# The loads of the running sequences' states are issued by GpSimd in place of SyncE

## The chip, the cores and the metric

The kernel runs on one core of one Trainium2 chip. The time is the device time of one execution in microseconds (us), as a median over several runs. Five engines work side by side, each through its own instructions in order: TensorE (PE), VectorE (DVE), ScalarE (ACT), GpSimd (POOL) and SyncE (SP). They wait for one another by semaphores. A transfer between the main memory and SBUF is issued by an instruction on one of the engines and then runs on 16 transfer engines.

## The reference

One layer of a hybrid decoder is computed for two inputs at once: a prompt of 512 new rows with 16 meta rows ahead, and eight running sequences of eight new rows each, which bring their states with them. The part that matters here is the state scan (SSD) of the running sequences: each sequence has for each of 32 heads a state of 64 x 128 numbers, which enters the outputs and is carried on.

```
def step(h, inp):
    x, d, bc, cc = inp
    cum = jnp.cumsum(d * a_g, axis=1)
    ...
    y = jnp.einsum('btsgh,bsghp->btghp', m, xdt)
    y = y + jnp.einsum('btgn,bghpn->btghp', cc, h) * jnp.exp(cum)[..., None]
    last = cum[:, -1]
    xw = xdt * jnp.exp(last[:, None] - cum)[..., None]
    h = h * jnp.exp(last)[..., None, None] + jnp.einsum('bsgn,bsghp->bghpn', bc, xw)
    return h, y
```

`h` starts as `state_ssm` of the sequence. Around the scan stand an input projection, pooling and convolution mixers, gates, an output projection and a feed-forward part, all in float32.

## The kernel before, in words

All 592 columns (16 meta, 512 prompt, 64 of the running sequences) lie transposed, features on partitions. Every product with a weight matrix is a `Unit`: the weights are loaded (line 95, tile `wr`, two buffers), split into a high part `wh` on ACT (line 113) and a low part `wl` on DVE (line 114), and multiplied in three passes (lines 119 to 121) into PSUM tiles `mm`. PE is fed with such units through the whole program, and the scan is woven between them: `weave` puts the steps of `ssd_steps(g)`, g = 0 to 3, between the units in program order. So there are four groups of eight heads each, in the text the first to the fourth. A scheduler then orders the instructions of each engine by its own estimate of when they can run.

In one group the steps that touch the change are these. `local(c)` loads the running sums of one chunk of rows (`cumD`, line 709), combines them on DVE (line 712), takes eight exponentials on ACT (line 714), multiplies them with the scores (DVE line 720), and reads the scores' PSUM tile a last time on ACT (line 723). `carry(c)` multiplies the chunk's operands (PE line 773). The PSUM tiles `px` that all these products and transposes use come from a ring of five, so a product may have to wait until an engine has read an older tile. `sample_load(u)`, u = 0 and 1, loads the states of four sequences in four transfers of 256 KB, each 128 partitions by four rows of 512 bytes, into two tiles `t` (line 793): the first and the second load of the group. `sample_turn(u)` transposes them on PE (line 804) into PSUM and copies them out on ACT (line 805). `sample_in`, `sample_add` and `sample_out` use them; `sample_out` scales the loaded states in place (ACT line 861), adds the new part (DVE line 862) after the products of line 857, and stores them (line 864). The tiles `t` come from a ring of nine buffers that the whole scan shares, so each load waits until the buffer's last reader is done.

GpSimd's own work in this stretch is small: it clears and fills the edges of the convolution's tiles `ext` (lines 630 and 631, three buffers), saves their ends (line 637), adds the carried part to the outputs (line 783) and adds up squares (line 926). All loads and stores but four stand in SyncE's queue.

Of the kernel before, what the change touches and what calls it, by code (L numbers as in the profile page):

```python
# [35 lines left out]
def hybrid_step(  # L36
# [8 lines left out]
    V, S, G, PE, DMA = nc.vector, nc.scalar, nc.gpsimd, nc.tensor, nc.sync  # L45
# [14 lines left out]
    def slot(shape, dt=F32):  # L60
        return sp.tile(shape, dt, tag="T", bufs=9, name=nm("t"))
# [618 lines left out]
    def rows_of(state, b, hs):  # L680

        return state[0, b, hs].rearrange("h p n -> (h p) n").rearrange("(j q) n -> q j n", q=128)

    def ssd_steps(g):

        hs = slice(8 * g, 8 * g + 8)
# [100 lines left out]
        def sample_load(u):  # L787

            h0s = []
            for i in range(2):  # L790
                t = slot([128, 2, 4, 128])
                for b in range(2):
                    DMA.dma_start(out=t[:, b], in_=rows_of(state_ssm, 4 * u + 2 * i + b, hs))
                h0s.append(t)
            st["h0", u] = h0s

# [84 lines left out]
        for c in range(1, 5):  # L881
            u = (c - 1) // 2
            if c % 2:
                steps.append(go(sample_load, u))
            if c < 4:
                steps.append(go(local, c))
            steps += [go(ahead, c), go(inside, c - 1)]
            if c % 2:
                steps += [go(sample_turn, u), go(carry, c - 1), go(sample_x, u)]
            else:  # L890
                steps += [go(sample_in, u), go(carry, c - 1), go(sample_add, u), go(sample_out, u)]
# [353 lines left out]
    for h in range(2):  # L1245
        for m in (6, 7):
            u = last[m]
# [35 lines left out]
```

## Time and profile before

| | us |
|---|---|
| runs, median of 3 | 1240.4 |
| runs, lowest and highest | 1239.92 and 1241.38 |
| the profiled execution, its own time | 1237.16 |
| the profiled execution, its span | 1235.4 |
| TensorE busy in the span | 1215.4 |
| VectorE busy in the span | 778.0 |
| GpSimd busy in the span | 168.2 |

The span runs from the first to the last instruction. The time of an execution is a little longer than its span. Busy time of TensorE is that of its matmuls, which overlap one another in the pipeline; what counts here is where it is idle. Issues of transfers do not count as busy time of an engine.

### The profile page before, as it was taken

The page shows a single profiled execution, that of the slowest core. Times are in us where ns is not written, and L with a number is a line of the kernel's source. Part 1 is how long each engine was busy: PE and PEld are TensorE (multiplying, and loading weights), DVE is VectorE, ACT ScalarE, POOL GpSimd, SP SyncE. Part 2 cuts the span into 40 slices and gives each one's busy share as a digit, 9 for nine tenths or more (in the row PEclk, how much of TensorE's full clock was granted, in tenths as well). Part 3 has the DMA queues.
Part 4 walks back from the last instruction along what each step waited for, and adds up shares of the span by engine and source line. Part 5 has one row for each costly group of instructions (what it writes and reads, how often), then busy time and mean ns, then how long its engine had stood idle before and what let it go on. Part 6 is the DMA issues. An engine that isn't in the chain of part 4 may idle for free.

```text
span 1235.4 us, 22605 instructions
## 1 busy us (share of the span) xinstructions
PE 1215.4 (98%) x9148; PEld 1176.3 (95%) x9148; DVE 778.0 (63%) x1372; ACT 557.0 (45%) x1164; POOL 168.2 (14%) x325
## 2 busy tenths in 40 slices
PE   8999999999999999999999999999999999999996
PEld 6999999899899989989999999999999999999996
DVE  6875347578888989787743344367676325677634
ACT  5435343545566577566442224344334113334333
POOL 2410000012013013011100001321212000111100
PEclk8999999999999999999999999999999999999999
DMA  6334426662634455654553542223322223222322
GB/s 187 109 78 123 117 89 192 173 184 51 185 115 122 135 164 141 178 151 140 156 146 100 170 139 70 69 69 103 103 69 70 85 86 103 68 69 85 113 74 77
DMA packets 174456, 143.99 MB, mean 117 GB/s; under 512 B 11630, under 2 KB 163854, under 8 KB 174345
## 3 DMA queue, kind: packets, MB, share of 16 engines
q1 hardware_dynamic: 173969, 142.40, 39.2%
q8 instruction: 72, 1.18, 0.4%
q14 instruction: 31, 0.25, 0.1%
q10 hardware_dynamic: 384, 0.16, 0.0%
HBM read 122.42 MB, written 20.34 MB: 116 GB/s over the span
## 4 chain that ended last, share of the span: by engine, by line
PE 92%; DMA 4%; ACT 2%; DVE 1%; SPq 1%; issue 0%; ACTq 0%; DVEq 0%
PE mm L119 27%; PE mm L121 27%; PE mm L120 27%; DMA t<-in_x_prompt_dram 1%; PE px L764 1%; PE px L742 1%; DMA t<-in_state_ssm_dram 1%; PE px L773 1%; DMA t<-cumD 1%; PE px L804 1%; ACT t L714 1%; PE px L817 1%; PE px L857 1%; PE px L726 1%; PE px L119 1%; PE px L121 1%
## 5 line engine op out<-in xcount | busy, mean ns | idle before, releaser
L119 PE MATMUL mm<-s,wl 128*128 128x288 f32 (+5 forms) x2528 | 759.4, 300 | 1.9 <-ACT s L297 1.4
L120 PE MATMUL mm<-s,wh 128*128 128x288 f32 (+5 forms) x2528 | 750.9, 297 | 0.0
L121 PE MATMUL mm<-s,wh 128*128 128x288 f32 (+5 forms) x2272 | 677.2, 298 | 0.0
L119 PEld LDWEIGHTS mm<-s,wl 128*128 128x128 f32 (+1 forms) x2528 | 476.0, 188 | 8.6 <-issue 5.3
L120 PEld LDWEIGHTS mm<-s,wh 128*128 128x128 f32 (+1 forms) x2528 | 476.1, 188 | 3.9 <-issue 3.3
L121 PEld LDWEIGHTS mm<-s,wh 128*128 128x128 f32 (+1 forms) x2272 | 427.3, 188 | 1.9 <-issue 1.4
L114 DVE TENSOR_TENSOR wl<-wr,wh 128x1024 fp32r<-128x1024 f32 (+2 forms) x165 | 198.5, 1203 | 169.5 <-ACT wh L113 169.0
L113 ACT ACTIVATE wh<-wr 128x1024 fp32r<-128x1024 f32 (+2 forms) x165 | 170.5, 1033 | 239.8 <-PE mm L121 196.7
L121 PE MATMUL mm<-t,wh 128*128 128x290 f32 (+1 forms) x256 | 76.0, 297 | 0.0
L1131 DVE SCALAR_TENSOR_TENSOR acc<-ext,ffT,acc 128x592 f32<-128x592 f32 x88 | 74.2, 844 | 1.7 <-ACT acc L1129 0.2
L642 DVE SCALAR_TENSOR_TENSOR acc<-ext,scT,acc 128x616 f32<-128x616 f32 x72 | 63.4, 880 | 1.9 <-ACT acc L640 1.4
L714 ACT ACTIVATE t<-t,TK 128x128 f32<-128x128 f32 (+1 forms) x160 | 48.5, 385 | 22.9 <-DVE t L712 22.9
L926 POOL TENSOR_TENSOR sqs<-sqs,acc 128x578 f32<-128x578 f32 x19 | 31.3, 1648 | 142.1 <-ACT acc L925 76.7
L121 PEld LDWEIGHTS mm<-t,wh 128*128 128x128 f32 x256 | 48.1, 188 | 0.0
L1158 ACT ACTIVATE s<-ext 128x512 fp32r<-128x512 f32 (+1 forms) x44 | 17.1, 436 | 64.3 <-DVE ext L1154 64.3
L861 ACT ACTIVATE t<-t,spr 128x128 f32<-128x128 f32 x128 | 40.2, 394 | 7.9 <-PE px L804 7.7
L1122 DVE TENSOR_TENSOR ext<-mm,t 128x224 f32<-128x224 f32 x43 | 16.8, 391 | 40.7 <-PE mm L121 40.7
L783 POOL TENSOR_TENSOR s<-s,tmp 128x256 f32<-128x256 f32 (+1 forms) x32 | 35.0, 1113 | 53.3 <-DVE tmp L777 45.7
L1159 POOL TENSOR_TENSOR s<-ext,s 128x512 fp32r<-128x512 f32 (+1 forms) x44 | 37.3, 870 | 34.9 <-ACT s L1158 34.9
L1184 DVE TENSOR_TENSOR t<-t,mm 128x288 f32<-128x288 f32 (+2 forms) x30 | 13.6, 453 | 43.6 <-PE mm L121 43.4
L1125 POOL COPY t<-ext 128x18 f32<-128x18 f32 x44 | 11.4, 259 | 202.4 <-DVE ext L1123 202.3
L1129 ACT ACTIVATE acc<-ext,ffT 128x592 f32<-128x592 f32 x44 | 38.1, 869 | 1.6 <-DVE ext L1123 1.5
(290 smaller groups left out, 1269.7 us busy)
## 6 DMA issues: line engine op xcount, KB each, us to landing
wr<-in_w_in_dram SPq DMA_DIRECT2D x28, 1024.0 KB
wr<-in_w_up_dram SPq DMA_DIRECT2D x22, 1024.0 KB
t<-cumD SPq DMA_DIRECT2D x16, 512.0 KB
t<-in_state_ssm_dram SPq DMA_DIRECT2D x32, 256.0 KB
out_dram<-t SPq DMA_DIRECT2D x32, 256.0 KB
wr<-in_w_ssd_out_dram SPq DMA_DIRECT2D x8, 1024.0 KB
wr<-in_w_down_dram SPq DMA_DIRECT2D x8, 768.0 KB
wr<-in_w_in_dram SPq DMA_DIRECT2D x10, 512.0 KB
```

The source lines that it names most:

```text
L113: S.activation(wh[:, :kb, :n], wr, AF.Copy)
L114: V.tensor_tensor(wl[:, :kb, :n], wr, f(wh[:, :kb, :n]), ALU.subtract)
L119: PE.matmul(o, wl[:, k, :m], hi[:, a:b], start=first, stop=False)
L120: PE.matmul(o, wh[:, k, :m], hi[:, a:b], start=False, stop=False)
L121: PE.matmul(o, wh[:, k, :m], lo[:, a:b], start=False, stop=last)
L642: V.scalar_tensor_tensor(acc[:, 0:616], ext[:, k:k + 616], scT[:, kb, 24 + k:25 + k], acc[:, 0:616], op0=ALU.mult, op1=ALU.add)
L714: S.activation(seg[:q, h, :q], seg[:q, h, :q], AF.Exp, scale=-1.0, bias=sums_[:, h:h + 1])
L783: G.tensor_tensor(v, v, t1[:, 2 * i:2 * i + 2, :nt], ALU.add)
L861: S.activation(v[:, b], v[:, b], AF.Copy, scale=elS[:, 4 * u + 2 * i + b, 4 * g + j:4 * g + j + 1])
L1129: S.activation(acc[:, 0:w], ext[:, 0:w], AF.Identity, scale=ffT[:, kb, 16:17], bias=ffT[:, kb, 19:20])
L1131: V.scalar_tensor_tensor(acc[:, 0:w], ext[:, k:k + w], ffT[:, kb, 16 + k:17 + k], acc[:, 0:w], op0=ALU.mult, op1=ALU.add)
L1159: G.tensor_tensor(l, a, f(h), ALU.subtract)
```

## The change

The four transfers of `sample_load` are issued by `G` (GpSimd) and no longer by `DMA` (SyncE).

```
             for i in range(2):
                 t = slot([128, 2, 4, 128])
                 for b in range(2):
-                    DMA.dma_start(out=t[:, b], in_=rows_of(state_ssm, 4 * u + 2 * i + b, hs))
+                    G.dma_start(out=t[:, b], in_=rows_of(state_ssm, 4 * u + 2 * i + b, hs))
                 h0s.append(t)
             st["h0", u] = h0s
```

Both queues are in order, so a load now waits its turn among other instructions than before, and the scheduler places some other instructions anew. Three places show it.

SyncE in the second group, around the group's first load. `wr_4076` is a block of weights, `t_3762` and `t_3765` are the two tiles of states, `t_3768` and `t_3981` are running sums of the chunks:

```order
 L709 DMA t_3662<-cumD 128x1024
 L95 DMA wr_4076<-in_w_in_dram 128x8x256
-L793 DMA t_3762<-in_state_ssm_dram 128x4x128 x2
-L793 DMA t_3765<-in_state_ssm_dram 128x4x128 x2
 L709 DMA t_3768<-cumD 128x1024
 L754 DMA t_3864<-ecumD 64x4x128 x2
+L709 DMA t_3981<-cumD 128x1024
 L95 DMA wr_4183<-in_w_in_dram 128x8x256
```

The running sums now follow the weights directly, and the next ones come ahead of the next weights. In the first group it is alike: the running sums stood behind the weights, the four loads of states and a store of line 608; now they stand behind the weights and one load of line 604, ahead of that store.

GpSimd in the third group, around the group's first load (`t_4923` and `t_4926`); `ext` with a number is a tile of the convolution:

```order
 L631 COPY ext_5329<-scT 128x8x3
 L637 COPY s_1167<-ext_5004 128x27
+L793 DMA t_4923<-in_state_ssm_dram 128x4x128 x2
+L793 DMA t_4926<-in_state_ssm_dram 128x4x128 x2
 L630 MEMSET ext_5579 128x3
 L631 COPY ext_5579<-scT 128x8x3
```

The four issues stand behind the copy of line 637 and ahead of the next tile's filling. In the second group they stand directly behind the filling of line 631, in the fourth directly behind an addition of line 783.

TensorE in the second group, where the product of line 773 (into `px_3969`, whose buffer in the ring was that of the next chunk's scores, read last by ACT at line 723) stands in a unit of 24 matmuls on the tile `mm_4009`:

```order
 L119 MATMUL mm_4009<-s_97,wl_3861 128x296
 L120 MATMUL mm_4009<-s_97,wh_3860 128x296
+L773 MATMUL px_3969<-t_3678 128x512
+L716 MATMUL px_3992<-s_2992 128x128
+L717 MATMUL px_3992<-ident,s_2992 128x128
+L726 MATMUL px_3999<-ident,s_3206 128x128 x2
+L726 MATMUL px_3999<-ident,s_3207 128x128 x2
 L121 MATMUL mm_4009<-s_101,wh_3860 128x296
```

The product moved from near the end of the unit to near its beginning. Most of the transposes of line 804 moved ahead too, in the second, third and fourth groups.

## Rows read from the trace of the kernel before

**Rows 1.** The page's head: span, and busy time of each engine.
```profile
span 1235.4 us, 22605 instructions
...
PE 1215.4 (98%) x9148; PEld 1176.3 (95%) x9148; DVE 778.0 (63%) x1372; ACT 557.0 (45%) x1164; POOL 168.2 (14%) x325
```
**Rows 2.** Stretches: length, busy time per engine, granted clock, DMA share, GB/s.
```profile
190.00:592.00 402.00, 396.19 (x3049) 368.22 (x3049) 320.65 (x578) 240.58 (x571) 61.14 (x102) 1.00 0.54 151
326.00:329.00 3.00, 3.00 (x24) 3.00 (x23) 3.00 (x4) 1.80 (x7) 0.00 (x0) 1.00 0.02 5
...
427.00:438.00 11.00, 9.78 (x83) 9.16 (x82) 8.84 (x19) 6.48 (x18) 0.23 (x1) 1.00 0.86 240
```
**Rows 3.** Waits of PE, 190 to 592 us: total, times, longest.
```profile
PE px L804 <- DMA t<-in_state_ssm_dram: 3.7, 3, 2.1
PE px L804 <- ACT t L723: 1.2, 1, 1.2
...
PE px L773 <- ACT t L723: 0.2, 1, 0.2
```
**Rows 4.** PE's timeline: start, length, instruction, [idle before it, releaser].
```profile
224.14 0.66 PE L804 MATMUL px<-ident,t 128*128 128x128 f32 x4 [1.16 <-ACT t L723]
...
336.31 0.63 PE L804 MATMUL px<-ident,t 128*128 128x128 f32 x4 [2.11 <-DMA t<-in_state_ssm_dram]
...
343.62 0.30 PE L120 MATMUL mm<-s,wh 128*128 128x296 f32 x1
...
434.86 0.63 PE L804 MATMUL px<-ident,t 128*128 128x128 f32 x4 [1.22 <-DMA t<-in_state_ssm_dram]
...
525.13 0.63 PE L804 MATMUL px<-ident,t 128*128 128x128 f32 x4 [0.38 <-DMA t<-in_state_ssm_dram]
```
**Rows 5.** SyncE's timeline around the first loads of the groups.
```profile
206.99 3.67 SPq L793 DMA_DIRECT2D t<-in_state_ssm_dram  x4
...
213.34 0.99 SPq L709 DMA_DIRECT2D t<-cumD  x1
...
329.16 4.80 SPq L793 DMA_DIRECT2D t<-in_state_ssm_dram  x4
334.02 1.22 SPq L709 DMA_DIRECT2D t<-cumD  x1
...
426.98 4.26 SPq L793 DMA_DIRECT2D t<-in_state_ssm_dram  x4
...
518.17 4.64 SPq L793 DMA_DIRECT2D t<-in_state_ssm_dram  x4
```
**Rows 6.** Pieces of the chain that ended last: start, length, work.
```profile
305.90 0.93 PE px L857 x4
...
562.65 1.81 PE px L804 x16
```
**Rows 7.** All of lines 793 and 783: ns min/median/max, first and last start.
```profile
L793 SPq DMA_DIRECT2D t<-in_state_ssm_dram x32: 438/540/2057, 207.0 to 547.3; - x32
...
L783 POOL TENSOR_TENSOR s<-s,tmp x32: 247/1118/2921, 249.6 to 588.9; 128x256 f32<-128x256 f32 x24, 128x32 f32<-128x32 f32 x8
```
**Rows 8.** Waits of SyncE's queue at line 604 for stores.
```profile
SPq L604 <- DMA mAD<-ext: 8.5, 4, 3.1
```
**Rows 9.** GpSimd's timeline: the instructions ahead of the moved loads.
```profile
323.32 0.21 POOL L631 COPY ext<-scT 128x24 f32<-128x24 f32 x1
...
428.88 0.23 POOL L637 COPY s<-ext 128x27 f32<-128x27 f32 x1 [6.41 <-ACT ext L634]
...
503.65 1.59 POOL L783 TENSOR_TENSOR s<-s,tmp 128x32 f32<-128x32 f32 x2 [7.58 <-ACT ext L645]
```
**Rows 10.** The second group's chain (timeline), and line 861's group (page).
```profile
340.82 1.23 DVE L712 TENSOR_TENSOR t<-t,TK 128x1024 f32<-128x1024 f32 x1 [2.95 <-DMA t<-cumD]
...
346.29 0.26 ACT L723 ACTIVATE t<-px 128x128 f32<-128x128 f32 x1
...
L861 ACT ACTIVATE t<-t,spr 128x128 f32<-128x128 f32 x128 | 40.2, 394 | 7.9 <-PE px L804 7.7
```

More of the change, by code (lines that the diff above doesn't have):

```diff
@@ L792, in sample_load @@
                 for b in range(2):
-                    DMA.dma_start(out=t[:, b], in_=rows_of(state_ssm, 4 * u + 2 * i + b, hs))
+                    G.dma_start(out=t[:, b], in_=rows_of(state_ssm, 4 * u + 2 * i + b, hs))
                 h0s.append(t)
```

## The prediction

> **What bounds the kernel now.** The page's head comes first [rows 1]: TensorE (PE) is busy for 1215.4 of 1235.4 us in 9148 instructions, one every 0.13 us; GpSimd (POOL) has 14%. So the time can change only where PE stands still. The table by stretches gives PE 396.19 us of the 402 in which the four groups of the state scan run, at full granted clock [rows 2]: 5.8 us of idle time, which is all that this stretch could give back. What PE waits for there is in the table of waits [rows 3]: 3.7 us in three waits for the state loads, before the transposes of line 804; 1.2 us once at the same line for ACT at line 723; 0.2 at line 773. PE's timeline places them [rows 4]: the states 2.11 us ahead of 336.31 (second group), 1.22 ahead of 434.86 (third), 0.38 ahead of 525.13 (fourth), ACT ahead of 224.14 (first). The three belong to a group's first load of states. SyncE's queue shows why these are late [rows 5]: the states leave right behind a load of weights (line 95), which waits for its own buffer, at 329.16, 426.98 and 518.17. Their buffers had been free for long: the products of line 857, the last readers, end at 306.83 for the load of 329.16 [rows 6].
>
> **The change, part by part.** It moves 32 transfers of 256 KB from SyncE's queue to GpSimd's. The bytes and buffers are the same. What moves is the place in two in-order queues, and with it PE's order, which the scheduler rewrites.
>
> *The cost of an issue on GpSimd.* No trace here has one; call it d. From below: SyncE's own, 0.44 us at least and 0.54 in the median [rows 7]. From above: the longest instruction of GpSimd among those that run beside VectorE in this stretch, 2.92 us, against a median of 1.12 for the same line [rows 7]. I take 1.1, because an issue on GpSimd is an instruction of that engine and the median is what it mostly takes; both ends stay in the range.
>
> *First group.* The states were no bound here, and GpSimd's place for them lies ahead of SyncE's 206.99. What moves is the running sums: cumD was issued at 213.34, behind the four issues of states (3.67 us) and a store [rows 5]. In the new order it follows the weights and one load of line 604. That load waits for a store to land; the longest such wait was 3.1 us [rows 8]. So cumD goes by 206.99 + 3.1 + 0.3 = 210.4 at the latest, 2.9 us earlier, and 1.05 MB of states no longer run beside it. The chain behind cumD ends in line 723, and the fourth four of transposes needs the PSUM tile that this line reads last: 1.16 us of waiting [rows 4]. 2.9 covers it. **-1.2.**
>
> *Second loads of each group.* These wait for a product of PE in both queues, so they leave when they left before. The last was issued by 547.8 (start 547.3 plus one issue) and is read at 562.65 [rows 6, 7]: about 15 us, against at most 4 x 2.92 + 1.1 = 12.8. Zero.
>
> *Second group, first load.* GpSimd is free for it at 323.32 + 0.21 = 323.53 [rows 9], 5.6 us before SyncE was. The transfer engines were nearly empty from 326 to 329 (share 0.02) [rows 2]. At the 240 GB/s of the third group's crowded stretch [rows 2], 256 KB take 1.09 us and the whole load 4.4, so even if it only begins at 326 it is there at 330.4. PE came to the transposes at 336.31 - 2.11 = 334.2; the new order puts them five matmuls earlier, at 333.5, and the second half of the tiles is wanted at about 335.1. The wait of 2.11 us goes; this holds up to d = 2.6 (323.5 + 4d + 1.1 = 335.1).
>
> *What is late next there.* The new order puts the product of line 773 nineteen matmuls earlier, directly behind the one that started at 343.62; without the wait of 2.11 PE is there at 343.92 - 2.11 = 341.8. It needs the PSUM tile that ACT frees at line 723, and that ended at 346.55, at the end of a chain that began with cumD: line 712 started at 340.82, after waiting 2.95 us for it [rows 10]. So the chain takes 5.7 us. cumD stood behind the four state issues on SyncE (334.02). Now it follows the weights at once: 1.57 MB at 240 GB/s from about 329.7 are there at 336.2. ACT is fuller at that time: thirteen scalings of line 861 at 0.3 us each (40.2 us for 128) [rows 10] stand between 333.9 and 337.8, 0.4 us past the end of line 712, and another 0.2 I allow behind. The chain ends at 342.5, and PE waits 0.7 us. Net for this group: -2.1 + 0.7 = **-1.4**.
>
> *Third group, first load.* Here GpSimd is the later one. The load stands behind a copy (line 637) that waits for ACT and runs at 428.88 to 429.11 [rows 9]; SyncE issued at 426.98 [rows 5]. And the new order of PE asks sooner: the first transposes three matmuls earlier than 433.64, at 433.25, the third four only six matmuls and two fours of transposes on. The engines move 240 GB/s from 427 to 438 [rows 2], 2.6 MB: weights (1.05), states (1.05), cumD (0.52), and before, the states came ahead of cumD. With two queues I let them take equal turns from 430 on: half the states are there at 430 + 0.52 / 0.12 = 434.3, the other half with the last byte, at 438. PE waits 1.0, then works 1.5, and waits from 435.8 to 438: 3.2 in all against 1.22. Net **+2.0**. If the states ran ahead of cumD instead, cumD would come last, the chain behind it would end as before, and the product of line 773, which moved ahead here as well, would wait for it: about the same sum. d does not enter until 429.1 + 4d + 1.1 passes 438, at d = 1.95; from there each us of d costs 4.
>
> The Trainium skill says in "DMA: Bandwidth & Descriptors", section "Issuing engines are not separate DMA queues", that transfers from all issuing engines run on the same 16 engines and interleave, and that issuing from several saves only issue time. The share of 0.86 from 427 to 438 agrees [rows 2]. By that rule the third group is as summed; the second gains all the same, as its engines stood empty.
>
> *Fourth group, first load.* The addition before it in GpSimd's queue ends at 503.65 + 1.59 = 505.24 [rows 9], 13 us before SyncE's issue. The 0.38 goes: **-0.4**. cumD leaves SyncE some 4.6 us earlier, the length of the four issues [rows 5], so the chain to line 773 is early too.
>
> The sum is -1.2 - 1.4 + 2.0 - 0.4 = -1.0 us. The profiled execution took 1237.16 us (span 1235.4); that makes 1236.2. The median of the runs is 1240.4, so I forecast 1239.4: **no change**. About 0.2%, 2.5 us, is what a measurement can tell here.
>
> **Rivals.** *Faster:* in the third group the bytes come sooner than I sum them: the engines' share there was 0.86 and not 1, so some of the 11 us was empty, and with two issuers more is in flight. If that keeps the wait of 1.2 as it is, the sum is -3.0: 1237.4 us. At best both its wait and the 0.7 at line 773 are gone too: -1.2 - 2.1 - 1.2 - 0.4 = -4.9, 1235.5. For it: the share of 0.02 ahead of the second group shows how soon an early load is over. Against it: GpSimd issues 2.1 us later than SyncE just there.
>
> *Slower, by the issue:* descriptors written by GpSimd are held up like its other work. The same tensor operation of line 783 takes 1.12 us mostly and 2.92 at worst [rows 7]. At 2.92 the third group's second half is there at 441.9, 3.9 us later than summed; the second group's at 336.3, 1.2 late. Sum -1.0 + 3.9 + 1.2 = +4.1: 1244.5. It decides from d = 2.7, where -1.0 + 4 x (2.7 - 1.95) + 4 x (2.7 - 2.6) reaches 2.4. The Trainium skill has a rule that speaks for this rival, in "SBUF — State Buffer", section "SBUF: two separate sides": while VectorE runs an operation in a mode that takes both ports, GpSimd cannot write descriptors, and a transfer of 620 ns becomes 3100 ns. By that figure, an estimate, d is 3.1 and the sum near +5. Whether VectorE's operations here are of that kind no run so far shows.
>
> *Slower, by the order:* PE's rewritten order asks in the second group for line 723's tile 4.7 us before ACT gave it up before (341.8 against 346.55). If cumD comes no earlier, because the states now share the transfer engines with it, PE waits 4.7 instead of 0.7: +4.0, 1243.4. The empty engines before 329 speak against it.
>
> That the change does not do what it says is excluded: the order shows all 32 issues on GpSimd.
>
> **How the numbers follow.** No change 0.52; faster 0.28; slower by the issue 0.13; slower by the order 0.07. So faster 0.28, same 0.52, slower 0.20. The range runs from the best of the faster case to the worse slow one, 1235.5 to 1244.5; the likeliest case alone, with d anywhere below 2.7 and turns of any kind, is 1237.9 to 1242.9.
>
> **What would show it.** In the changed kernel's trace: d as the length of an issue on GpSimd; no wait for ACT at line 804 near 222; no wait of PE for states near 333 and 524; one of about 3 us near 434; a short wait at line 773 for ACT near 342; line 712 of the second group starting near 336 and not 341; SyncE without the 4 us of state issues behind the weights. Wrong, if issues take over 2 us, if line 773 waits for more than 2 us, or if states still land last where the engines were empty.

## The result, and the profile after

The changed kernel takes 1246.15 us (median of 6, 1244.87 to 1247.7), the kernel before 1239.86 (median of 6, 1239.05 to 1241.38). The ratio is 1.0055 (95% interval 1.0046 to 1.0065): slower by 6.3 us, and outside the predicted range. The profiled execution took 1246.6 us (span 1244.9). The one of before was a quick one for its kernel (1237.16), so the two profiles differ by 9.4 us where the medians differ by 6.3.

What PE waits for from 190 to 600 us (line waited at, releaser, total, times, longest); it answers to [rows 3]:

```profile
PE px L804 <- DMA t<-in_state_ssm_dram: 4.9, 1, 4.9
PE px L804 <- issue: 3.9, 2, 2.0
PE px L804 <- ACT t L723: 1.0, 1, 1.0
PE px L742 <- DVE t L720: 0.5, 1, 0.5
```

PE's timeline places them, as [rows 4] did before:

```profile
223.18 0.66 PE L804 MATMUL px<-ident,t 128*128 128x128 f32 x4 [0.97 <-ACT t L723]
...
341.58 0.99 PE L804 MATMUL px<-ident,t 128*128 128x128 f32 x4 [1.98 <-issue]
...
438.62 1.09 PE L804 MATMUL px<-ident,t 128*128 128x128 f32 x4 [4.88 <-DMA t<-in_state_ssm_dram]
...
529.80 1.09 PE L742 MATMUL px<-t,t 128*64 128x128 f32 x16 [0.52 <-DVE t L720]
...
538.38 0.63 PE L804 MATMUL px<-ident,t 128*128 128x128 f32 x4 [1.96 <-issue]
```

The states are late in the third group alone, and there by 4.88 us instead of 1.22. In the second and fourth groups a stop of 2 us has taken the place of the wait for states. It stands before the last four of the group's sixteen transposes, and the trace names no releaser for it ("issue"). VectorE's timeline in the second group names it:

```profile
337.94 1.23 DVE L712 TENSOR_TENSOR t<-t,TK 128x1024 f32<-128x1024 f32 x1 [2.46 <-DMA t<-cumD]
339.08 0.85 DVE L642 SCALAR_TENSOR_TENSOR acc<-ext,scT,acc 128x616 f32<-128x616 f32 x1
339.85 0.34 DVE L746 SCALAR_TENSOR_TENSOR s<-s,spr,px 128x128 f32<-128x128 f32 x1
340.11 0.86 DVE L642 SCALAR_TENSOR_TENSOR acc<-ext,scT,acc 128x616 f32<-128x616 f32 x1
340.88 0.60 DVE L746 SCALAR_TENSOR_TENSOR s<-s,spr,px 128x128 f32<-128x128 f32 x2
```

The fourth four of transposes needs the PSUM tile that the additions of line 746 read. The last of them ends at 341.48, and PE goes on at 341.58. They stand in VectorE's queue behind line 712, which waited 2.46 us for cumD. Before, the scheduler had them ahead of line 712, which started at 340.82 [rows 10]:

```profile
337.52 0.34 DVE L746 SCALAR_TENSOR_TENSOR s<-s,spr,px 128x128 f32<-128x128 f32 x1
```

With each of the three stops the granted clock falls to the lower level, 1.2 GHz (in the third group it falls while PE still stands). In the table by stretches (length, busy times, granted clock, DMA share, GB/s) the kernel before showed 1.00 [rows 2], and read microsecond by microsecond it is 1.00 from 190 to 600; now:

```profile
342.00:345.00 3.00, 3.00 (x14) 3.00 (x13) 2.62 (x5) 3.00 (x9) 0.25 (x2) 0.50 0.00 0
...
439.00:442.00 3.00, 3.00 (x16) 2.97 (x15) 0.67 (x3) 1.97 (x6) 0.00 (x0) 0.50 0.06 18
...
539.00:542.00 3.00, 3.00 (x17) 3.00 (x16) 2.19 (x3) 3.00 (x11) 0.00 (x0) 0.61 0.00 0
```

PE is busy there, but at 0.5 three us do about the work of 1.5. How much each group lost is read from its second set of transposes, which wait for nothing in either kernel. PE's timeline of before, first of each group:

```profile
271.55 1.64 PE L804 MATMUL px<-ident,t 128*128 128x128 f32 x13
...
372.57 0.66 PE L804 MATMUL px<-ident,t 128*128 128x128 f32 x4
...
468.69 0.66 PE L804 MATMUL px<-ident,t 128*128 128x128 f32 x4
...
562.51 1.95 PE L804 MATMUL px<-ident,t 128*128 128x128 f32 x16
```

and of the changed kernel:

```profile
271.51 1.75 PE L804 MATMUL px<-ident,t 128*128 128x128 f32 x14
...
373.02 1.09 PE L804 MATMUL px<-ident,t 128*128 128x128 f32 x8
...
474.52 0.66 PE L804 MATMUL px<-ident,t 128*128 128x128 f32 x4
...
572.16 1.95 PE L804 MATMUL px<-ident,t 128*128 128x128 f32 x16
```

The changed kernel stands at 0.0, +0.5, +5.8 and +9.7 us: the first group cost nothing, the second 0.5, the third 5.4, the fourth 3.8.

GpSimd's timeline shows the issues themselves (compare [rows 9]):

```profile
323.83 2.98 POOL L793 DMA_DIRECT2D t<-in_state_ssm_dram  x4 [0.34 <-issue]
...
429.99 2.98 POOL L793 DMA_DIRECT2D t<-in_state_ssm_dram  x4 [0.39 <-issue]
...
511.55 2.99 POOL L793 DMA_DIRECT2D t<-in_state_ssm_dram  x4
```

and the row of line 793 answers to [rows 7] (ns, shortest, median and longest):

```profile
L793 POOL DMA_DIRECT2D t<-in_state_ssm_dram x32: 747/749/967, 191.3 to 556.5; - x32
```

An issue takes 0.75 us, at most 0.97. So d was not the cost.

### The profile page after: what moved, and what is told of

Its sections match the earlier page's. It is cut to its first block, busy times and chain, and to the rows that moved or that the text cites. A ratio compares the mean times of both kernels' runs of the same rounds, so it can differ in the third digit from the quotient of the medians.

```text
span 1244.9 us, 22649 instructions
## 1 busy us (share of the span) xinstructions
PE 1218.8 (98%) x9148; PEld 1181.4 (95%) x9148; DVE 780.8 (63%) x1372; ACT 556.9 (45%) x1164; POOL 193.8 (16%) x357
## 4 chain that ended last, share of the span: by engine, by line
PE 91%; DMA 3%; DVE 2%; issue 1%; ACT 1%; SPq 0%; ACTq 0%; POOL 0%; DVEq 0%; POOLq 0%
PE mm L119 27%; PE mm L121 27%; PE mm L120 27%; DMA t<-cumD 2%; PE px L804 1%; PE px L764 1%; PE px L742 1%; PE px L773 1%; DMA t<-in_state_ssm_dram 1%; PE px L817 1%; PE px L857 1%; PE px L119 1%; PE px L121 1%; PE px L120 1%; DMA al<-in_a_log_dram 0%
## 5 line engine op out<-in xcount | busy, mean ns | idle before, releaser
L712 DVE TENSOR_TENSOR t<-t,TK 128x1024 f32<-128x1024 f32 (+1 forms) x20 | 25.2, 1259 | 25.5 <-DMA t<-cumD 23.9
```

## The experiments

**How the order is held.** Most runs hold the order of an engine's instructions, so that only one thing differs. A list of instruction names for each engine, from the first to the last place where the two kernels differ, is turned into edges between neighbours; an edge fixes the order of issue and adds no wait:

```
+    def keep_order():
+        ...
+                if last is not None:
+                    tc.add_manual_dep(i, last.name,
+                                      mybir.DependencyInfo(mybir.DependencyClass.NoSync, mybir.DependencyReason.DATA),
+                                      reason="order")
+                last = i
+        ...
+    keep_order()
```

"Old" is the order of the kernel before, "new" that of the changed one. The theory: the rewritten order costs the second and fourth groups, the late landing the third. The rival: GpSimd's queue costs, and the order is innocent.

**Loads on GpSimd, old order.** The line of the change, with PE, VectorE, ScalarE and SyncE held in the old order, GpSimd in the new one:

```
-                    DMA.dma_start(out=t[:, b], in_=rows_of(state_ssm, 4 * u + 2 * i + b, hs))
+                    G.dma_start(out=t[:, b], in_=rows_of(state_ssm, 4 * u + 2 * i + b, hs))
```

> All state loads on GpSimd as in the changed kernel, but the instructions of TensorE, VectorE, ScalarE and SyncE are held in the order of the kernel before. Theory (the rewritten order costs most of it in the second and fourth groups, the late landing in the third): the 2.1 us wait of the second group and the 0.4 of the fourth go and no wait for VectorE takes their place; the third group's states still land near 438, so PE waits about 4 us there instead of 1.2, and some 1.5 to 2 us more go to a lower clock behind that stop. Sum about +2: near 1242, ratio 1.001 to 1.003. Rival (the order is innocent, GpSimd's queue alone costs): as the changed kernel, +6, ratio 1.005.

Measured 1238.14, ratio 0.9987 (0.9979 to 0.9996). The same queue and the same loads are no slower than before once the order is the old one. Of the waits for states only the third group's is left, followed by a clock of 0.50 from 435 to 437:

```profile
434.04 0.59 PE L804 MATMUL px<-ident,t 128*128 128x128 f32 x3 [2.51 <-DMA t<-in_state_ssm_dram]
```

The rival falls. The sum was 3.5 us too high: 1.5 of that is the wait, which came out at 2.5 and not 4; where the rest lies stays open.

**Loads on SyncE, new order.** The kernel before, with the rows of the changed kernel on every engine and the loads behind the weights as ever:

> The loads stay on SyncE, at their places behind the weights, but all other instructions of every engine are held in the order of the changed kernel. Theory: as slow as the changed kernel or slower, 1244 to 1248, with waits of 1 to 3 us before the fourth four of transposes (line 804) in the second and fourth groups, for the additions of line 746, which stand on VectorE behind line 712 and so behind cumD. Rival (GpSimd's queue alone costs): no difference from the kernel before, 1240.

Measured 1248.55, ratio 1.0069 (1.0057 to 1.0082). The order alone, with no load on GpSimd, costs as much as the change; the two intervals overlap. As the loads stay behind the weights, the new order meets late states too: PE waits 5.1 us for them, in four places. Its timeline shows both kinds of stop one after the other:

```profile
338.53 0.63 PE L804 MATMUL px<-ident,t 128*128 128x128 f32 x4 [2.90 <-DMA t<-in_state_ssm_dram]
...
346.68 0.52 PE L804 MATMUL px<-ident,t 128*128 128x128 f32 x3 [1.60 <-issue]
...
541.42 0.97 PE L804 MATMUL px<-ident,t 128*128 128x128 f32 x4 [2.38 <-issue]
```

**Nine additions.** The changed kernel, all orders held as they are, but on VectorE (here the second group):

```
 L642 SCALAR_TENSOR_TENSOR acc_3850<-ext_3843,scT,acc_3850 128x616
-L746 SCALAR_TENSOR_TENSOR s_3206<-s_3206,spr,px_3867 128x128
+L746 SCALAR_TENSOR_TENSOR s_3206<-s_3206,spr,px_3867 128x128 x2
+L746 SCALAR_TENSOR_TENSOR s_3207<-s_3207,spr,px_3867 128x128 x2
 L712 TENSOR_TENSOR t_3768<-t_3768,TK 128x1024
```

> The changed kernel with all its orders held, but on VectorE nine additions of line 746 (second, third and fourth groups) go ahead of the line 712 that they stood behind. Theory A (these additions alone make the two stops of 2 us at line 804): both stops and the stretches at the lower clock behind them go, -7: 1239. Theory B (the stop only hides the next one in the same chain, cumD to line 712 to line 714 to line 720 to line 723): the waits at line 804 go, but PE then stands at line 773, about 1.4 us in the second group and 2.5 in the fourth; gain 0 to 3: 1243 to 1246.

Measured 1246.62, ratio 1.0051 (1.0039 to 1.0063): nothing gained, and 0.6 us above the range of theory B. The waits of PE are those of theory B:

```profile
PE px L773 <- ACT t L723: 5.3, 2, 2.9
PE px L804 <- DMA t<-in_state_ssm_dram: 5.2, 1, 5.2
```

The stop only moved to line 773, 2.45 us in the second group and 2.88 in the fourth. What is late is the chain behind cumD; which instruction meets it first doesn't matter.

**One engine's order at a time.** Two runs of the changed kernel: PE alone old, all else new; and PE new, VectorE and ScalarE old. The lists are given here by the kernel that they come from:

```
+    KEEP: PE from before; ACT, DVE, SP, POOL from after
...
+    KEEP: PE, SP, POOL from after; ACT, DVE from before
```

> The changed kernel with every engine held in the changed order, except TensorE, which is held in the order of before. Theory (either rewritten order alone is enough for a stop, since both wait for the same chain behind cumD): in the second and fourth groups PE still stands before a four of transposes (line 804), for the additions that VectorE holds behind line 712, some 2.5 to 3 us; time within 2 us of the changed kernel, 1244 to 1248. Rival (PE's order alone is the cause): as the run in the old order, 1238 to 1240.

> The changed kernel with VectorE and ScalarE held in the order of before; TensorE, GpSimd and SyncE as changed. Theory as in the run beside it: PE stands at line 773 for ScalarE's line 723, 2 to 3 us in the second and fourth groups, and about 4 us for states in the third; 1243 to 1247. Rival (VectorE's order alone is the cause): 1238 to 1240.

Measured 1248.87, ratio 1.0083 (1.0067 to 1.0099), and 1262.08, ratio 1.0189 (1.0173 to 1.0205). A stop stays when TensorE alone has the old order, and when VectorE and ScalarE have it, as the theory had it. SyncE's order is the new one in both, and no run gives it alone. But in the second group line 712 starts 9.2 and 9.6 us after the load of weights in these runs, 9.5 in the changed kernel and 9.4 with all old orders (first run), so SyncE's new order did not make cumD later there. The first time lies 0.9 us above its range; the second is far above it, and how much of that comes from mixing two orders, no run tells. The rows of both, PE's timeline with the old PE order:

```profile
340.01 0.63 PE L804 MATMUL px<-ident,t 128*128 128x128 f32 x4 [2.96 <-issue]
```

and with the new one beside the old VectorE order:

```profile
345.74 1.41 PE L773 MATMUL px<-t 128*128 128x512 f32 x2 [3.77 <-ACT t L723]
```

With the old VectorE and ScalarE orders beside PE's new one the chain is later still (8.0 us from the start of line 712 to the end of line 723 in the second group, 5.4 in the changed kernel), so PE stands at line 773 in three groups (9.2 us in all), and four stretches at the lower clock follow stops.

**The third group: earlier, in the new order.** The changed kernel, all orders held, with one move on GpSimd:

```
+L793 DMA t_4923<-in_state_ssm_dram 128x4x128 x2
+L793 DMA t_4926<-in_state_ssm_dram 128x4x128 x2
 L637 COPY s_1167<-ext_5004 128x27
-L793 DMA t_4923<-in_state_ssm_dram 128x4x128 x2
-L793 DMA t_4926<-in_state_ssm_dram 128x4x128 x2
```

> The changed kernel with all its orders held, but the third group's first load is ahead of the copy of line 637 in GpSimd's queue. Theory (the late landing costs 4.9 us and the lower clock behind it about 2): -6, 1240, and the stops of 2 us in the second and fourth groups stay. Rival (in the new order the third group too runs into the chain behind cumD, so that another wait takes the place): -2 or less, 1244.

Measured 1242.87, ratio 1.0021 (1.0009 to 1.0033). No wait for states is left, and 3.3 us are gained, between the two: as the rival said, the third group now has a stop of its own for the additions of line 746, 1.63 us.

**The third group: another second queue.** Old order, and the third group's first load on ScalarE:

```
-                    G.dma_start(out=t[:, b], in_=rows_of(state_ssm, 4 * u + 2 * i + b, hs))
+                    (S if (g, u) == (2, 0) else G).dma_start(out=t[:, b], in_=rows_of(state_ssm, 4 * u + 2 * i + b, hs))
```

> As the run in the old order, but the third group's first load is issued by ScalarE behind line 640, about when GpSimd issued it (427.4). Theory (GpSimd's queue begins late, 3 us after the issue, and gives way to SyncE's): from ScalarE the first bytes come 1 to 1.5 us after the issue and share with SyncE's at once; the wait for states falls from 2.5 us to about 1, and 1 to 3 us are gained over that run: 1235 to 1237. Rival (any second queue comes behind what is already in flight): the wait stays at 2.5, 1238.

Measured 1238.7, ratio 0.9989 (0.9981 to 0.9998). My theory of GpSimd's queue falls: from ScalarE, issued from 427.20, the states are as late:

```profile
434.82 0.41 PE L804 MATMUL px<-ident,t 128*128 128x128 f32 x2 [2.91 <-DMA t<-in_state_ssm_dram]
```

The queues of this run between 427 and 430.8 us (packets, MB, share) hold SyncE's alone:

```profile
q1 hardware_dynamic: 959, 1.20, 99.8%
```

and from 430.8 to 436.5 ScalarE's q10:

```profile
q10 hardware_dynamic: 2108, 1.05, 67.0%
q1 hardware_dynamic: 79, 0.22, 10.6%
```

So a load that is issued from a second queue 2 us behind a megabyte of weights and half of one of cumD came behind them, whichever engine issued it.

**The place in the queue: early on GpSimd, early on SyncE.** Old order in both. First GpSimd with the move shown above; then no GpSimd at all, but on SyncE (here the second group, the same in all four):

```
-L95 DMA wr_4076<-in_w_in_dram 128x8x256
 L793 DMA t_3762<-in_state_ssm_dram 128x4x128 x2
 L793 DMA t_3765<-in_state_ssm_dram 128x4x128 x2
+L95 DMA wr_4076<-in_w_in_dram 128x8x256
```

> As the first run, and the third group's first load is moved ahead of the copy of line 637 in GpSimd's queue, so that it is issued near 422.5. Theory: its bytes begin about 2 us after the first issue, while SyncE's queue is empty, and are there near 429; no wait for states is left in any group: -2.1 - 1.2 - 0.4 = -3.7, 1236, ratio 0.997, and less if the kernel before loses time to a lower clock behind its stops. Rival (an issue on GpSimd or its slower transfers cost in themselves): no gain over the first run.

> The kernel before, all orders held, loads on SyncE, but the four first loads stand ahead of the load of weights (line 95) and no longer behind it. Theory (what matters is the place in a queue, not the engine that issues): no wait for states is left, cumD follows the weights at once; as the early loads on GpSimd, 1232 to 1235. Rival (GpSimd's own queue gives something): 2 us or more slower than those, 1236 to 1239.

Measured 1233.27, ratio 0.9952 (0.9939 to 0.9965), and 1233.47, ratio 0.9949 (0.9937 to 0.9961). Both gain 6 us, and the engine makes no difference. The first was expected at 1236, too little a gain: the sum took only the 3.7 us of waits for states [rows 3], which from the profiled 1237.16 give 1233.5; why the median of before is some 2.5 us longer than that execution stays open below. SyncE's timeline in the second run shows why it costs nothing: the queue had been standing for the weights' buffer with nothing else to do.

```profile
319.62 4.60 SPq L793 DMA_DIRECT2D t<-in_state_ssm_dram  x4
329.09 0.37 SPq L95 DMA_DIRECT2D wr<-in_w_in_dram  x1
```

**Four constraints.** The kernel before with four edges on SyncE, everything else left to the scheduler (the numbers are those of the last load of states and of the load of weights of each group):

```
+    KEEP: [2455, 2638], [3767, 4077], [4928, 5238], [6072, 6380]
```

> The kernel before with four constraints only: on SyncE, in each group, the load of weights (line 95) is queued behind the group's first load of states; everything else is ordered by the scheduler. Theory (with cumD too ahead of the weights the chain to line 723 is early, so a rewritten order does no harm): no wait for states or at line 773; 1233 to 1236, as the held version. Rival (the scheduler's new order brings a stop of its own, as it did in the change): 1238 to 1244.

Measured 1232.8, ratio 0.9953 (0.994 to 0.9966), faster than both kernels and as fast as the held versions. The scheduler rewrote the orders here too, but put cumD ahead of the weights with the states, so the chain is early. No wait for states and none at line 773 is left:

```profile
318.68 4.48 SPq L793 DMA_DIRECT2D t<-in_state_ssm_dram  x4
323.21 1.91 SPq L709 DMA_DIRECT2D t<-cumD  x1
327.85 0.37 SPq L95 DMA_DIRECT2D wr<-in_w_in_dram  x1
```

These orders are this run's own. No run gives the changed kernel's orders an early cumD.

**The kernel before, a second profile.** No edit.

> The kernel before, a second profile. Theory: the 2.1 us stop of the second group is followed by a stretch at the lower clock in some executions and not in others, which is why the profiled one took 1237.2 and the timed ones 1240; in this one, if its time is near 1240, the granted clock is below 1 behind a stop, for 3 to 4 us. Rival: the clock stays at 1.00 in the whole scan and the 2.7 us lie elsewhere.

Measured 1239.19 (one run). The theory fails: this execution has a stop of 2.35 us for states, and the granted clock stays at 1.00 behind it. Its waits are longer in several places instead (1.69 at line 804 for line 723, 1.37 for line 846). Why executions of one kernel differ by 2 us stays open.

## Why the prediction was wrong, by its steps

Three runs split the 6.3 us. With the old order and the third group's load early too, loads on GpSimd gain 6.4 us (1233.27 against 1239.68). The late load of the third group takes 4.9 of that back (1238.14). The rewritten orders cost another 8.0 (1246.15), and 8.9 with the loads on SyncE. The prediction had the signs of the first two and almost nothing for the third: 0.7 us at line 773.

*The cost of an issue* was taken as 1.1 us and is 0.75. The rule of the Trainium skill in "SBUF — State Buffer", section "SBUF: two separate sides", by which d would have been 3.1, did not show: the longest of 32 issues beside a busy VectorE took 0.97. Whether VectorE ran operations of the kind that the rule means, no trace tells. The rival that was given most of the slower chance was the wrong one.

*First group*, -1.2: the step "2.9 covers it" failed. cumD was issued at 210.17, as worked out, but landed only 0.8 us earlier than before (line 712 started at 217.85 against 218.69), and the wait of 1.16 became 0.97. The load of weights just ahead of it had left 2.2 us later than before (208.71 against 206.55), so cumD still came behind that megabyte. An earlier issue was not an equally earlier landing.

*Second group*, -1.4: the wait for states went, as forecast. The step "What is late next there" had the right chain and named it, cumD to line 723, but the wrong place and too small a size: 0.7 us at line 773, where 1.98 came at line 804. cumD landed at 337.9 and not at 336.2: the sum counted 1.57 MB, but SyncE's queue moved 1.83 from 328 to 338, with the two loads of line 754 among them. And the order of VectorE, which put line 746 behind line 712, was not read for this term; only PE's was. The fall of the clock behind the stop had no term at all. Measured +0.5, net of the 2.11 that went.

*Third group*, +2.0: the sign was right and the term mis-sized; measured 5.4. "I let them take equal turns" failed. The queues of the changed kernel from 430 to 434 us (packets, MB, share), with the four loads issued from 429.99 on:

```profile
q1 hardware_dynamic: 1040, 1.30, 100.1%
...
q0 software_dynamic: 2, 0.01, 1.1%
```

GpSimd's queue q0 moved 0.01 MB of 1.31 in these 4 us, and the rest from 434 to 440. About 2 of the 4 us are its way to the first bytes (in the second group it had moved 0.11 MB 2.2 us after its first issue), but from 432 to 434 it still moved 0.01 and SyncE's 0.65. Only then did the two share, 0.27 and 0.20 MB from 434 to 436. The sum had half of the states at 434.3 and all at 438; the queue had moved 0.76 of its 1.05 MB by 438. So PE could not even use the first half for its 1.5 us of work: 4.88 us of waiting instead of 3.2, and the lower clock behind. The rule of the Trainium skill in "DMA: Bandwidth & Descriptors", section "Issuing engines are not separate DMA queues", that transfers from all issuing engines interleave, is not borne out from 432 to 434; in the run with ScalarE's queue it was the same. The share of 0.86, which the prediction read as agreeing with it, was SyncE's queue alone. That an issuer of its own saves only issue time fits: the two early versions are equal.

*Fourth group*, -0.4: the step "so the chain to line 773 is early too" failed; measured +3.8. The early load was no gift here. GpSimd issued it at 511.55, ahead of the group's previous cumD (516.59 on SyncE), which then took 8.1 us from its issue to line 712, and 5.5 before (509.85 to 515.37), when the states came after it. From 515 to 519 GpSimd's queue moved 0.94 MB and SyncE's 0.44. The changed kernel's VectorE waits for it:

```profile
524.68 1.23 DVE L712 TENSOR_TENSOR t<-t,TK 128x1024 f32<-128x1024 f32 x1 [2.83 <-DMA t<-cumD]
525.83 1.22 DVE L114 TENSOR_TENSOR wl<-wr,wh 128x1024 fp32r<-128x1024 f32 x1
```

Line 114 stands behind it and ends at 527.05; it is what frees the weights' buffer, and SyncE's load of weights starts at 527.08, with the next cumD right behind it. Before, the weights went at 517.74. Of the 9.3 us between, 5.8 had been lost in the groups before; the rest is this cascade. It makes the chain late, but alone it does not stop PE. With the loads on GpSimd and the old order (first run) the same cumD is as late and the weights go at 521.29, yet PE waits only 0.26 and 0.23 us in that group:

```profile
510.86 0.51 SPq L709 DMA_DIRECT2D t<-cumD  x1
...
518.90 1.23 DVE L712 TENSOR_TENSOR t<-t,TK 128x1024 f32<-128x1024 f32 x1 [2.57 <-DMA t<-cumD]
```

The new order adds the stop: it puts four additions of line 746 behind the next line 712, which starts at 536.02, and at their end PE's wait of 1.96 at 538.38 ends. Before, they stood ahead of it.

The rival "slower, by the order" had the right mechanism for the second and fourth groups: a rewritten order that asks for the chain earlier than it comes. It was given 0.07, for one group alone, and refuted by the empty engines before 329. But cumD waited behind the load of weights in the old and in the new order, so empty engines before 329 could not help it. The run with four constraints, in which cumD passes the weights, agrees.

## What to carry to other kernels

Where a load is late behind another load that waits for its own buffer, move it ahead in its queue; here an engine of its own gained no more, and a second queue's load came behind the weights and running sums that the first had been given 2 to 3 us before. When a scheduler orders the instructions, one load on another queue can rewrite the order of every engine, and a wait moved forward on one of them can be enough: read for each engine what now stands behind the instruction that waits for the latest transfer. Price a stop of PE with the stretch at the lower clock that can follow.

## What the runs showed of the hardware

A stop of PE may or may not be followed by the lower clock. In the thirteen profiles it came with all six stops over 3 us in the scan, with 9 of 17 between 1.9 and 3 us, and with none of the shorter ones. PE ran 3 to 6 us at 1.2 GHz behind such a stop, which gave away 1.5 to 3 us. Two stops of the third group show the difference (length, busy times, granted clock, DMA share, GB/s), first behind the one of 2.51 us with the loads on GpSimd in the old order, then behind the one of 2.91 us with ScalarE's queue:

```profile
435.00:437.00 2.00, 2.00 (x11) 1.98 (x10) 0.39 (x1) 1.55 (x6) 0.00 (x0) 0.50 0.05 16
...
435.00:437.00 2.00, 2.00 (x18) 1.98 (x17) 0.76 (x1) 1.84 (x7) 0.00 (x0) 1.00 0.10 27
```

PE was busy in both, with 11 matmuls in the one and 18 in the other. What decides between like stops, no run here tells.
